# Four loads of the attention stage put behind group 4's transposing transfers (one-layer hybrid decoder step)

## The chip, the cores and the metric

The kernel runs on one core of a Trainium2 chip. The time is device microseconds from start to end of the program on that core, the median of the runs shown. TensorE is called PE, VectorE DVE, ScalarE ACT, GpSimd POOL and SyncE SP, as in the profile. All data is fp32; the large products are made of three fp32r passes (high times high, high times low, low times high).

## The reference, cut to what matters

```python
def _layer(x, ..., prompt):
    h = _rmsnorm(x, g_pre)
    z = h @ w_in                     # gates, conv inputs, queries, keys, values, memory queries
    ...
    conv = conv_w[0] * up[:, 0:t] + conv_w[1] * up[:, 1:t + 1] + conv_w[2] * up[:, 2:t + 2]
    out_a = jax.nn.silu(cg) * cb * conv
    ...
    out_b = jax.nn.silu(ag) * o_b    # o_b: sliding-window attention, window 128, a sink logit per head
    out_c = jax.nn.silu(mg) * o_c    # o_c: attention of 4 heads into 256 memory tokens
    y = jnp.concatenate([out_a, out_b, out_c], axis=-1) @ w_out
    return x + _rmsnorm(y, g_post), ...
```

There are 4096 prompt tokens and 64 sample tokens, a model width of 1024, 8 window heads over 2 key-value heads and 4 memory heads, all of head dimension 64.

## The kernel before, in words

The first part of the program, up to about 940 us, is the input projection. It leaves its products in DRAM: queries, keys and memory queries as high and low halves in `qd`, values in `vn`, and the gated convolution rows and gates in `md` (the "mix" rows, which the attention results multiply).

The second part runs over 33 blocks of output rows. **Block** i is 128 tokens; its output projection is 48 matmuls, 24 for each half of the 1024 columns (`y_0`, then `y_1`, line 1661). Queries, keys and mix rows are loaded by **chunks** of 256 tokens, two blocks each. The attention itself is done by **groups** of 128 tokens, group g belonging to chunk g // 2. Between the matmuls of block i the program places one attention step, `values_and_scores(i)`: the scores of group i + 3 (tiles `ws` and `xs`, matmuls at line 1128), then the values of group i + 1 (tile `pv`, same line), then the softmax of group i + 3 on DVE and ACT. The order on every engine is the order in which this code is written, the two DMA-issuing engines SP and POOL included.

What one group passes through after its softmax, and by which engine:

- `turn_band` and `turn_cross` (lines 1338 and 1342) transpose the weights in 32 x 32 squares on DVE. `turn_cross` then sends sixteen **transposing transfers** of 64 KB (`w<-s`, line 1345), which put the squares in their transposed places. For groups 3 and 4 the eight with odd k are kept in a list (`moves`) and are issued on POOL a little later, the eight with even k on SP at once. From group 5 on all sixteen are on SP.
- `masks` (line 1361, POOL) clears what lies outside the window. The values need its result.
- The values need also the chunk's mix rows (`load_mix`, line 1174, 1 MB into the tile `place` or `mix`; the product at lines 1375 and 1406 reads them) and two 128-token pieces of the values (`half_load`, line 1181, 64 KB, tiles `vh`).

The queries of a chunk are loaded by POOL in two halves, `load_queries(0)` and `load_queries(1)` (line 1166, tile `q<-qd`, 768 KB each: the high halves and the low ones); the keys by `load_keys` (line 1160, `kst<-qd`, 384 KB). Scores of a group need both halves of its chunk's queries from their first matmuls on.

A block's end is split in two tails that are placed in the next step: `tail(0)` computes the row's factor (`yst`; a power on POOL at line 1682), and `tail(1)` scales and adds the residual row `xr` (loaded by `block.load`, line 1616) and stores it (`o_yp<-xr`). For block 1 the scale and add are one DVE instruction at line 1697. The accumulator `y_1` of a block shares the PSUM tile `pv` with the values of the groups, and `y_0` shares a bank with the first scores; both are released by DVE's product with the gain (`yn`, line 1668) and ACT's square (line 1669).

Each kind of queue, SP's and POOL's, signals its transfers on eight semaphores in turn. A transfer waits on its engine for the transfer that used the same semaphore before it, which is the one eight places ahead of it in that kind of queue.

Of the kernel before, what the change touches and what calls it, by code (L numbers as in the profile page):

```python
# [26 lines left out]
NCH = 4096 // CT  # L27
# [24 lines left out]
def hybrid_layer(ctx: ExitStack, tc: tile.TileContext, a: dict):  # L52
# [1030 lines left out]
    chunks = {}  # L1083
# [23 lines left out]
    def psum(bank, name):  # L1107

        if ps is None:
            return third["ps"].tile([P, 512], F32, tag="m", name=name)  # L1110
        return ps[bank].tile([P, 512], F32, tag="b", name=name)
# [71 lines left out]
    class Group:  # L1183
# [32 lines left out]
        def scores(self):  # L1216
            self.open_scores()
            bands = [psum(n, f"ws{self.b}_{n}").rearrange("p (h k) -> p h k", h=2) for n in ((1, 2, 5, 4) if self.b == 4 else range(4))]
            cross_bank = lambda hh: psum(hh if self.b == 4 else 4 + hh, f"xs{self.b}_{hh}").rearrange("p (j k) -> p j k", j=2)
            if self.b != 4:  # L1220
                cross = [cross_bank(hh) for hh in range(2)]
            self.bands(bands[:2], 0)
            if self.b == 5:
                for fn in groups[4].moves:
                    fn()
            tail(0)
            if self.b == 4:
                turn(1, 3)
            loads = query_loads(self.b // 2 + 2)[:1] if self.b % 2 and self.b > 3 else query_loads(self.b // 2 + 1)[1:] if self.b > 4 else ()
            if self.b == 5:  # L1230
                loads.pop(0)()
            if self.b == 4:
                for fn in groups[3].moves:
                    fn()
                blocks[1].load()
                chunk_load(3)
            self.bands(bands[2:], 1)
            if self.b == 4:
                cross = [cross_bank(hh) for hh in range(2)]
            self.crosses(cross)  # L1240
            for fn in loads[:1]:
                fn()
            if self.b not in (4, 5):
                tail(1)
            for fn in loads[1:]:
                fn()
            if self.b == 3:
                blocks[1].split(0)
            self.band_softmax()
            return cross  # L1250
# [190 lines left out]
    def tail(part):  # L1441
        if part < len(tails):
            tails[part]()
        if part:
            tails.clear()

    def turn(part, g):
        if 3 <= g < 2 * NCH:
            (groups[g].turn_band, groups[g].turn_cross, groups[g].masks)[part]()

    def query_loads(c):
        if c >= NCH:
            return ()
        if c not in chunks:
            chunks[c] = Chunk(c)
        return [chunks[c].load_keys, lambda: chunks[c].load_queries(0), lambda: chunks[c].load_queries(1)]

    def chunk_load(c):
        for fn in query_loads(c):
            fn()  # L1460
# [255 lines left out]
    def events_of(i, block):  # L1716

        ev = {}

        def at(p, k, fn, *args):  # L1720
            ev.setdefault((p, k), []).append(lambda: fn(*args))

        if i < 2:
            at(1, 0, weights, i + 3)
        if i == 1:
            at(0, 0, turn, 0, 3)
        if i == 2:
            at(0, 0, turn, 0, 4)
            at(0, 0, turn, 1, 4)
        at(0, {0: 3, 1: 4}.get(i, 0), values_and_scores, i)  # L1730
        if i > 1:
            ev.setdefault((0, 0), []).insert(0, block.load)
        if i == 30:
            at(0, 5, blocks[32].split)
            at(1, 1, blocks[31].split)
            at(1, 6, blocks[31].load)
        if i % 2 == 0 and 2 < i < 2 * NCH - 2:
            at(0, 3, lambda: chunks[i // 2 + 1].load_mix())
        if i != 1:
            at(1, 1, turn, 2, i + 2)  # L1740
        if i == 1:
            at(0, 5, lambda: chunks[2].load_mix())
            at(0, 6, turn, 2, 3)
        if i > 0 and i + 3 < 2 * NCH:
            at(0, 5, half_load, i + 3)
        if i > 1:
            at(1, 2, turn, 0, i + 3)
            at(1, 2, turn, 1, i + 3)
        if i:
            if i + 1 < len(blocks) and blocks[i + 1].b != 32:  # L1750
                at(*((1, 3) if i < 28 else (0, 6)), blocks[i + 1].split, *((1,) if i == 1 else ()))
        for (n, p, k), stage in sample.items():
            if n == i:
                at(p, k, next, stage, None)
        return ev

    for i, block in enumerate(blocks):
        if block.b == 32:
            tail(0)
            tail(1)  # L1760
            blocks[32].load()
            for stage in (mem0, mem1, window):
                for _ in stage:
                    pass
        block.run(i == len(blocks) - 1, events_of(i, block) if i < 31 else {})
# [107 lines left out]
```

## Time and profile before

| | us |
|---|---|
| median of 3 runs (1471.61 to 1475.16) | 1474.47 |
| the profiled execution's own time | 1468.87 |
| its span, first to last instruction | 1467.1 |
| PE busy (matmuls) | 1453.7 |
| DVE busy | 1209.0 |
| ACT busy | 757.2 |
| POOL busy | 447.5 |

The 1.77 us between the profiled execution's time and its span lie before the first and after the last instruction. The mean granted TensorE clock is 0.999. The span is that of PE with few gaps: 13.4 us in which no matmul is under way. Times within the trace are given in us from the span's start.

### The profile page before, as it was taken

Reading aid. Unit: us, or ns where it says so; the run is one execution under the profiler, and the core shown is the slowest. Engines: PE = TensorE matmul, PEld = TensorE weight load, DVE = VectorE, ACT = ScalarE, POOL = GpSimd, SP = SyncE. Lnnn points to the kernel's source line nnn. Section 1 sums busy time; section 2 is a strip of 40 time slices with the busy share of each in tenths; the row PEclk is TensorE's granted clock in tenths of the full one; section 3 lists DMA queues with packets and bytes.
Section 4 is the critical chain, followed back from the end, with each engine's and each line's share of the span. In section 5 each row is a group of like instructions: output and inputs, shape, how many; then the busy total and the mean of one; then the engine's idle time right before and its main releaser. Section 6 shows DMA issues by size and latency. Waiting matters only on the chain.

```text
span 1467.1 us, 30934 instructions
## 1 busy us (share of the span) xinstructions
PE 1453.7 (99%) x11457; PEld 1335.7 (91%) x11457; DVE 1209.0 (82%) x1897; ACT 757.2 (52%) x1869; POOL 447.5 (31%) x622
## 2 busy tenths in 40 slices
PE   9999999999999999999999999999999999999998
PEld 9999999999999999999999999977777777777776
DVE  6779878899998877799677777988898889898853
ACT  6776655566522222244445544656656655655542
POOL 0222323312300000000002224265556566556561
PEclk9999999999999999999999999999999999999999
DMA  9989999887865644475977968999989898988772
GB/s 272 188 244 221 294 264 272 247 283 237 234 220 171 216 130 127 139 282 138 329 265 227 292 217 276 316 230 234 246 219 222 217 257 221 244 219 234 230 221 102
DMA packets 211980, 337.27 MB, mean 230 GB/s; under 512 B 55285, under 2 KB 125941, under 8 KB 211797
## 3 DMA queue, kind: packets, MB, share of 16 engines
q1 hardware_dynamic: 158901, 225.89, 52.0%
q0 software_dynamic: 44144, 78.68, 21.3%
q10 hardware_dynamic: 8784, 30.72, 6.8%
q8 instruction: 91, 1.49, 0.5%
q14 instruction: 60, 0.49, 0.1%
HBM read 192.48 MB, written 110.15 MB: 206 GB/s over the span
## 4 chain that ended last, share of the span: by engine, by line
PE 87%; DMA 5%; DVE 3%; SPq 2%; issue 1%; ACT 1%; POOL 1%; ACTq 0%; DVEq 0%; POOLq 0%
PE c L383 60%; PE y L1661 18%; PE pv L1128 4%; PE ws L1128 2%; SPq L1345 2%; DMA mix<-md 1%; DMA q<-qd 1%; PE xs L1128 1%; DMA qd<-z 1%; PE mem_acc L810 1%; DMA o_yp<-xr 1%; ACT s L1296 0%; DMA w<-s 0%; DMA xr<-in_x_p 0%; DMA vh<-vn 0%
## 5 line engine op out<-in xcount | busy, mean ns | idle before, releaser
L1661 PE MATMUL y<-wo,mh 128*128 128x512 f32 (+1 forms) x1040 | 328.7, 391 | 0.0
L390 DVE TENSOR_TENSOR z<-c,z 128x520 f32<-128x520 f32 (+1 forms) x308 | 193.2, 643 | 66.0 <-PE c L383 64.7
L1661 PEld LDWEIGHTS y<-wo,mh 128*128 128x128 f32 x1040 | 194.2, 188 | 52.4 <-DVE wmx L1286 5.0
L1661 PE MATMUL y<-wo,ml 128*128 128x512 f32 (+1 forms) x520 | 201.1, 387 | 0.0
L1330 POOL TENSOR_SCALAR s<-s,xrd 128x256 f32<-128x256 f32 x124 | 58.3, 482 | 199.5 <-DVE xrd L1325 193.9
L1661 PEld LDWEIGHTS y<-wo,ml 128*128 128x128 f32 x520 | 97.8, 188 | 18.5
L1296 ACT ACTIVATE s<-s,wnm 128x128 f32<-128x128 f32 x256 | 98.7, 387 | 0.0
L756 POOL MEMSET negs<- 128x1 f32 x1 | 0.1, 100 | 285.1 <-DMA md<-cacc 285.1
L1273 ACT COPY s<-ws 128x256 f32<-128x256 f32 x128 | 41.2, 378 | 76.4 <-PE ws L1128 66.1
L1691 POOL TENSOR_TENSOR xr<-yn,xr 128x1024 f32<-128x1024 f32 x29 | 69.4, 2394 | 17.9 <-ACT yn L1690 17.7
L1361 POOL TENSOR_SCALAR_AFFINE_SELECT wd<-w 128x512 f32<-128x512 f32 x64 | 59.4, 928 | 36.0 <-DMA w<-s 19.6
L1669 ACT ACTIVATE y<-y 128x512 f32<-128x512 f32 (+1 forms) x66 | 38.6, 585 | 60.8 <-DVE yn L1668 60.5
L1128 PEld LDWEIGHTS ws<-kst,q 64*128 64x128 f32 x768 | 47.7, 186 | 12.1 <-issue 9.2
L1319 ACT ACTIVATE s<-xs,xnm 128x256 f32<-128x256 f32 x128 | 58.0, 459 | 0.0
L1668 DVE TENSOR_TENSOR yn<-y,gpost 128x512 f32<-128x512 f32 (+1 forms) x66 | 44.7, 678 | 16.1 <-PE y L1661 15.0
L1361 POOL TENSOR_SCALAR_AFFINE_SELECT w<-w 128x512 f32<-128x512 f32 x64 | 56.5, 902 | 2.2
L1128 PE MATMUL ws<-kst,q 64*128 64x256 f32 x768 | 55.0, 288 | 1.0 <-ACT y L1669 1.0
L1277 DVE COPY_PREDICATED s<-wmask,ws 128x256 f32<-128x256 uint8 x124 | 47.9, 440 | 8.9 <-ACT s L1273 6.5
L392 ACT COPY z<-c 128x520 f32<-128x520 f32 (+1 forms) x44 | 24.3, 555 | 58.8 <-PE c L383 54.6
L296 ACT ACTIVATE nat<-nat 104x1024 f32<-104x1024 f32 x40 | 42.3, 1057 | 21.8 <-DMA nat<-in_x_p 21.8
L1296 ACT ACTIVATION_READ_ACCUMULATOR s<-s,wnm 128x1 f32 x256 | 47.9, 187 | 0.0
L187 POOL DMA_DIRECT2D md<-th x48 | 26.3, 549 | 70.2 <-DVE th L444 38.5
(968 smaller groups left out, 4970.9 us busy)
## 6 DMA issues: line engine op xcount, KB each, us to landing
w<-s SPq DMA_DIRECT2D x456, 64.0 KB
q<-qd POOLq DMA_DIRECT2D x32, 768.0 KB
xr<-in_x_p SPq DMA_DIRECT2D x32, 512.0 KB
nat<-in_x_p SPq DMA_DIRECT2D x39, 416.0 KB
o_yp<-xr SPq DMA_DIRECT2D x31, 512.0 KB
md<-th POOLq DMA_DIRECT2D x48, 260.0 KB
qd<-zh SPq DMA_DIRECT2D x48, 260.0 KB
qd<-z SPq DMA_DIRECT2D x48, 260.0 KB
```

What stands on the lines that cost most here:

```text
L296: S.activation(t[:RG], t[:RG], AF.Square, accum_out=r[:RG, i : i + 1])
L383: TE.matmul(bank[:, :HW], l, r, start=first and i == 0, stop=last and i == 3 * KH - 1)
L390: add = lambda dst, other: V.tensor_tensor(dst, c, other, op=ALU.add)
L1128: ins = TE.matmul(o, w, x, **kw)
L1277: V.copy_predicated(to, squares(third["wmask"]), squares(s3[:, :, 0:P]))
L1296: S.activation(sm[:, h], sm[:, h], AF.Exp, bias=nm[:, h : h + 1], scale=SCALE, accum_out=den[:, h : h + 1])
L1319: S.activation(p[:, i], s[:, i].rearrange("p (a k j) -> p a k j", a=2, k=4), AF.Exp, bias=nm[:, i : i + 1], scale=SCALE, accum_out=den[:, ...
L1330: G.tensor_scalar(p[:, i], p[:, i], rd[:, i : i + 1], 0.5, op0=ALU.mult, op1=ALU.mult)
L1361: G.affine_select(out, src, pattern=[[32 * sign, 2], [0, 8], [sign, 32]], compare_op=op, fill=0.0, base=base * sign, channel_multiplier=-s ...
L1661: TE.matmul(acc, self.hl[l][:, k], wo[k][c0 // 512][:, r, c0 % 512 : c0 % 512 + c1 - c0], start=j == 0, stop=j == passes * KT - 1)
L1668: V.tensor_tensor(yn[:m, c0:c1], acc[:m], gpost[0][:m, c0:c1], op=ALU.mult)
L1691: total = G.tensor_tensor(self.xr, yn, self.xr, op=ALU.add)
```

## The change

Five edits, all in the steps of blocks 1 and 2:

- `load_queries(1)` of chunk 3 was issued on POOL in group 4's scores (step 1). It is now issued in group 5's scores (step 2), behind group 4's eight transfers on POOL.
- `load_keys` of chunk 4 was issued at that place in group 5's scores; it is now issued after the cross scores of that group.
- `load_mix` of chunk 2 and `half_load(4)` were issued on SP in step 1. They are now issued at the start of step 2, behind group 4's eight transfers on SP.
- `block.load` of block 2 (its residual row) was SP's first instruction of step 2, ahead of group 4's transfers. It is now behind them and behind the two loads above.
- No other step issues anything at another place.

```diff
@@ Group.scores
             if self.b == 5:
-                loads.pop(0)()
+                chunks[3].load_queries(1)
             if self.b == 4:
                 for fn in groups[3].moves:
                     fn()
                 blocks[1].load()
-                chunk_load(3)
+                for fn in query_loads(3)[:2]:
+                    fn()
@@ events_of
         if i == 2:
             at(0, 0, turn, 0, 4)
             at(0, 0, turn, 1, 4)
+            at(0, 0, half_load, 4)
+            at(0, 0, lambda: chunks[2].load_mix())
+            at(0, 0, block.load)
         at(0, {0: 3, 1: 4}.get(i, 0), values_and_scores, i)
-        if i > 1:
+        if i > 2:
             ev.setdefault((0, 0), []).insert(0, block.load)
...
         if i == 1:
-            at(0, 5, lambda: chunks[2].load_mix())
             at(0, 6, turn, 2, 3)
-        if i > 0 and i + 3 < 2 * NCH:
+        if i > 1 and i + 3 < 2 * NCH:
             at(0, 5, half_load, i + 3)
```

SP's queue, from group 3's transfers to block 1's end, before (`w_12385` is group 3's, `w_12563` group 4's; `xr_12402` and `xr_12559` are the residual rows of blocks 1 and 2, `xr_12190` block 0's; `place` takes chunk 2's mix rows):

```order
L1345 DMA w_12385<-s_12204 32x512 x8
L1616 DMA xr_12402<-in_x_p 128x1024
L1698 DMA o_yp<-xr_12190 128x1024
L1174 DMA place<-md 128x8x256
L1181 DMA vh_12499<-vn 128x128
L1616 DMA xr_12559<-in_x_p 128x1024
L1345 DMA w_12563<-s_12361 32x512 x8
L1698 DMA o_yp<-xr_12402 128x1024
L1181 DMA vh_12714<-vn 128x128
```

The same stretch of SP's queue in the changed kernel, whose line numbers are one higher there (`w_12557` is group 4's, `xr_12569` block 2's residual row):

```order
L1346 DMA w_12385<-s_12204 32x512 x8
L1617 DMA xr_12402<-in_x_p 128x1024
L1699 DMA o_yp<-xr_12190 128x1024
L1346 DMA w_12557<-s_12361 32x512 x8
L1181 DMA vh_12566<-vn 128x128
L1174 DMA place<-md 128x8x256
L1617 DMA xr_12569<-in_x_p 128x1024
L1699 DMA o_yp<-xr_12402 128x1024
L1181 DMA vh_12714<-vn 128x128
```

Three loads moved from ahead of group 4's eight transfers to behind them; nothing else changed places.

POOL's queue before, from group 3's transfers to the loads of chunk 4's keys (`q_12406` and `kst_12404` are chunk 3's, `kst_12606` chunk 4's; `yst_12346` is block 1's factor):

```order
L1345 DMA w_12385<-s_12204 32x512 x8
L1160 DMA kst_12404<-qd 128x2x384
L1166 DMA q_12406<-qd 128x6x256 x2
L1361 AFFINE_SELECT wd_12504<-w_12385 128x512
L1361 AFFINE_SELECT wd_12504<-w_12385 64x512
L1361 AFFINE_SELECT w_12385<-w_12385 128x2x256 x2
L1345 DMA w_12563<-s_12361 32x512 x8
L1682 TENSOR_TENSOR yst_12346<-yst_12346,mhalf 128x1
L1160 DMA kst_12606<-qd 128x2x384
```

The same stretch of POOL's queue in the changed kernel (`kst_12634` is chunk 4's):

```order
L1346 DMA w_12385<-s_12204 32x512 x8
L1160 DMA kst_12404<-qd 128x2x384
L1166 DMA q_12406<-qd 128x6x256
L1362 AFFINE_SELECT wd_12500<-w_12385 128x512
L1362 AFFINE_SELECT wd_12500<-w_12385 64x512
L1362 AFFINE_SELECT w_12385<-w_12385 128x2x256 x2
L1346 DMA w_12557<-s_12361 32x512 x8
L1683 TENSOR_TENSOR yst_12346<-yst_12346,mhalf 128x1
L1166 DMA q_12406<-qd 128x6x256
L1160 DMA kst_12634<-qd 128x2x384
```

The second half of chunk 3's queries moved from ahead of group 4's eight transfers to behind them and behind block 1's factor; the transfer eight places ahead of the last of the eight is now the first half of the queries and no longer the second.

## The prediction

> **What bounds the kernel now.** I read first how busy each engine is: PE's matmuls cover 99% of the span, so only what lets PE wait, or adds to it, can move the time.
>
> ```profile
> PE 1453.7 (99%) x11457; PEld 1335.7 (91%) x11457; DVE 1209.0 (82%) x1897; ACT 757.2 (52%) x1869; POOL 447.5 (31%) x622
> ```
>
> The span is 1467.1 us, so 13.4 us hold no matmul. The view of waits, for PE alone, tells which of them have a releaser (engine, line waited for, us in total, times, longest).
>
> ```profile
> PE pv L1128 <- ACT y L1669: 3.8, 4, 2.3
> PE ws L1128 <- ACT y L1669: 1.0, 1, 1.0
> ```
>
> The first scores of a group and the values of a group wait for ACT's square of a block's output, which frees the PSUM tile. Where this happens is read in order of time from PE's weight loads: the score and value rows of steps 2 to 6, that is the scores of groups 5 to 9. The number ahead of the arrow is the idle time before the row.
>
> ```profile
> 964.55 1.49 PEld L1128 LDWEIGHTS ws<-kst,q 64*128 64x128 f32 x24 [0.35 <-ACT s L1328]
> 981.59 1.49 PEld L1128 LDWEIGHTS ws<-kst,q 64*128 64x128 f32 x24 [1.45 <-ACT y L1669]
> 986.30 0.85 PEld L1128 LDWEIGHTS pv<-w,mv 128*64 128x64 f32 x16 [2.49 <-ACT y L1669]
> 999.90 1.49 PEld L1128 LDWEIGHTS ws<-kst,q 64*128 64x128 f32 x24 [0.35 <-issue]
> 1002.68 0.85 PEld L1128 LDWEIGHTS pv<-w,mv 128*64 128x64 f32 x16 [0.57 <-ACT y L1669]
> 1016.30 1.49 PEld L1128 LDWEIGHTS ws<-kst,q 64*128 64x128 f32 x24 [0.35 <-issue]
> 1018.64 0.85 PEld L1128 LDWEIGHTS pv<-w,mv 128*64 128x64 f32 x16
> 1032.25 1.49 PEld L1128 LDWEIGHTS ws<-kst,q 64*128 64x128 f32 x24 [0.35 <-issue]
> ```
>
> From 1016.30 to 1032.25 a step without a wait takes 15.95 us, and its values start 2.34 us after its scores. The three steps before it take 17.04, 18.31 and 16.40 us, so they lose 1.09, 2.36 and 0.45 us: **3.90 us in all**. That is the most that this change can gain at the place it touches.
>
> What makes ACT late there stands in the chain that ended last (start, us, what).
>
> ```profile
> 960.23 15.34 DMA q<-qd
> ...
> 975.84 0.25 POOL w L1345
> ...
> 976.35 0.59 POOL yst L1682
> 976.97 1.29 DVE xr L1697
> ...
> 980.17 0.60 DVE yn L1668
> 980.85 0.47 ACT y L1669
> ```
>
> The second half of chunk 3's queries, issued at 960.23, lands at 975.57. POOL's last transposing transfer of group 4 waits for it, because it stands eight software transfers behind it; behind it on POOL stands block 1's factor, behind that on DVE the residual addition at line 1697, and behind that the `yn` that frees block 2's accumulators.
>
> **The change part by part.** First POOL (start, length, instruction, idle before it).
>
> ```profile
> 968.22 3.51 POOL L1345 DMA_DIRECT2D w<-s  x7 [0.76 <-DVE s L1277]
> 975.84 0.50 POOL L1345 DMA_DIRECT2D w<-s  x1 [4.12 <-DMA q<-qd]
> 980.22 1.84 POOL L1330 TENSOR_SCALAR s<-s,xrd 128x256 f32<-128x256 f32 x4 [2.56 <-DVE xrd L1325]
> 983.08 2.36 POOL L1361 TENSOR_SCALAR_AFFINE_SELECT wd<-w 128x512 f32<-128x512 f32 x2 [1.02 <-DMA w<-s]
> 985.51 1.40 POOL L1361 TENSOR_SCALAR_AFFINE_SELECT w<-w 128x512 f32<-128x512 f32 x2
> 987.41 0.91 POOL L1166 DMA_DIRECT2D q<-qd  x1
> 991.07 0.86 POOL L1166 DMA_DIRECT2D q<-qd  x1
> ```
>
> With the second query half gone from ahead, the eighth transfer waits for the first half, which was issued one place earlier in the old order. Keys and first half are 1152 of the 1920 KB that had landed after 15.34 us, so by the same rate they are in about 9.2 us after 960.23, at 969.4 and likely earlier, since the other half and the mix rows no longer compete. The eight transfers then run from 968.22 for 8 x 0.50 us to 972.2, block 1's factor is ready 0.59 us later at 972.8, and the moved query load is issued at 972.8. It adds nothing to POOL's work. The keys of chunk 4 come one place later in POOL's order, 0.9 us, for scores that begin at 1016.30; I take nothing for them.
>
> Now DVE, and in the last row ACT.
>
> ```profile
> 973.09 0.17 DVE L1313 TENSOR_SCALAR xnm<-xmx 128x2 f32<-128x2 f32 x1
> 976.97 1.29 DVE L1697 SCALAR_TENSOR_TENSOR xr<-yn,yst,xr 128x1024 f32<-128x1024 f32 x1 [3.71 <-POOL yst L1682]
> 980.09 0.67 DVE L1668 TENSOR_TENSOR yn<-y,gpost 128x512 f32<-128x512 f32 x1
> 983.26 1.60 DVE L1636 TENSOR_TENSOR ml<-mix,mh 128x1024 fp32r<-128x1024 f32 x1
> 984.79 0.68 DVE L1668 TENSOR_TENSOR yn<-y,gpost 128x512 f32<-128x512 f32 x1
> ```
>
> ```profile
> 985.56 0.58 ACT L1669 ACTIVATE y<-y 128x512 f32<-128x512 f32 x1 [1.65 <-DVE yn L1668]
> ```
>
> DVE is free at 973.26, and the factor is there at 972.8. The whole row of DVE work behind it moves up by the 3.71 us that DVE now waits. The first `yn` goes from 980.09 to 976.4 (block 2's first half ends on PE half an output projection before 980.5, at about 975, so its data is there), and the first scores of group 6 find their bank free: **1.09 us** gained. The second `yn` goes from 984.79 to 981.1, after PE's end of block 2 at 964.55 + 15.95 = 980.50. The values started 1.51 us after that `yn` (986.30 less 984.79), so they may start at 982.6; unhindered PE comes to them at 980.50 + 2.34 = 982.84. That is **2.36 us** more, with 0.25 us in hand. What is late next is the same square one step on, the 0.45 us before 1002.68; its DVE chain moves with PE, and I leave it.
>
> The masks must not become the wait instead. POOL's scaling at 980.22 moves up by 3.71 to 976.5 and ends at 978.4; masks of 3.8 us follow until 982.2, while PE reads the first masked tile 0.85 us into the values, at 983.7. For that group 4's transfers must land by 978.4. On SP they are freed as follows.
>
> ```profile
> 961.19 0.65 SPq L1174 DMA_DIRECT2D place<-md  x1
> 961.89 4.26 SPq L1181 DMA_DIRECT2D vh<-vn  x1
> 969.41 0.33 SPq L1616 DMA_DIRECT2D xr<-in_x_p  x1
> 970.11 10.56 SPq L1345 DMA_DIRECT2D w<-s  x8
> 983.41 10.04 SPq L1345 DMA_DIRECT2D w<-s  x16
> ```
>
> Before, SP held block 2's load until 969.41 and then took 10.56 us for eight transfers. Group 5's sixteen took 10.04, or 0.63 each. In the new order the eight start when DVE has transposed, near POOL's 968.2, and take 8 x 0.63 = 5.0 us, to 973.2: 7.4 us earlier than 980.67. POOL's `wd` at 983.08 shows the old ones landed 2.4 us after the last issue; so about 975.6, 2.8 us before they are needed. I take nothing for the masks; the bounds are nothing and, if they landed as late as before, the old 2.4 us.
>
> The three loads now behind them: the 64 KB of values have from 973.2 to 983.7. The mix rows are issued at about 973.8 and needed by DVE after the values, past 985. SP's next instruction stood 4.26 us behind the mix rows' issue, so block 2's residual row goes out at about 978; it is needed only at block 2's end, by a POOL addition near 986. Nothing on PE waits for that addition directly. I take 0 for the three; the upper bound is 15.34 us to land, as the query half took, which puts the mix rows at 989: DVE some 2 us late in a step where it has more slack than that before the next `yn`.
>
> The one load with a near deadline is **the second query half**: issued at 972.8, needed by the first scores of group 6 at 980.50, so 7.7 us. Here the queues' traffic helps (packets, MB, share of the sixteen engines): the first two rows are 970 to 975, when this half ran beside the mix rows; the last two are the software queue in 996 to 997 and 997 to 998, when the same load for chunk 4, issued at 991.07, came to its end.
>
> ```profile
> q1 hardware_dynamic: 922, 0.95, 68.9%
> q0 software_dynamic: 549, 0.69, 50.2%
> ...
> q0 software_dynamic: 118, 0.11, 63.1%
> q0 software_dynamic: 2, 0.00, 1.5%
> ```
>
> The later load took 6 us from issue to end: by that row it lands at 978.8. At the 0.138 MB per us of the shared stretch its 0.79 MB need 5.7 us, plus the time to its first packet. The far end is the 15.34 us of the old order, where those 1152 KB stood in front. I take 6 us, the row of a load with nothing large ahead of it, and so no wait; 15.34 us would mean 988.1 and a wait of 7.6 us. The Trainium skill (DMA: Bandwidth & Descriptors, Anatomy of one DMA) gives a software transfer 2.0 us plus its bytes at 436 GB/s, an estimate of 3.8 us for this one. By that it lands at 976.6 and the sum is the same; the row at 991.07 with its 6 us does not agree, and decides.
>
> **The sum**: 1.09 + 2.36 = 3.45 us less. Against the profiled execution that is 1468.87 - 3.45 = 1465.4. That execution was 5.6 us under the median of the runs shown, so for the median I say 1474.47 - 3.45 = **1471.0**.
>
> **The rivals.**
> *The query half lands late.* Between 980.50 and 983.95 it eats the gain and the time lies between 1471.0 and 1474.5. For it: it shares with the mix rows and group 4's last transfers, and has 1.7 us in hand. The Trainium skill (DMA: Bandwidth & Descriptors, Rules for kernel authors) says to issue a transfer early and wait for it late; the change does the opposite with this one, and by that rule the time would go this way. The trace bears it out only for what something waits for soon: this is the one such load.
> *Slower.* The same load landing after 983.95, 11.1 us past its issue, costs more than both waits returned; at the old 15.34 us the time is 1474.47 + 7.6 - 3.45 = 1478.6. Against it: no row shows such a load that slow without another one ahead of it.
> *The wait stays.* If POOL's eighth transfer found the first query half still under way until 975, or the masks took the place of the square, the time would be 1473.5 to 1474.5. Against it: the 9.2 us above.
> *More than the profile shows.* The runs shown are 2.7 to 6.3 us slower than the profiled one. If part of that is these same waits, longer, up to 3 us more go: 1468.
>
> **How the numbers follow.** Forecast 0.64, late but not slower 0.14, slower 0.08, wait stays 0.07, more 0.07. A measurement of this kernel tells about 0.3% (4.4 us) from no change, and the forecast's 3.45 us are 0.23%, so it counts as within, but scatter may carry a seventh of it over. Faster by over 0.3%: 0.07 + 0.09 = 0.16. Slower by over 0.3%: the far part of the slower case and some scatter, 0.06. Within: 0.78. The range takes in the profiled basis, 1465.4, and the late landings up to about 1477.
>
> **What would show it.** Right: POOL's eight transfers unbroken from about 968, line 1698 (1697 before) on DVE near 973.3, score rows of groups 6 and 7 some 16 us apart, SP's eight in 5 us. Wrong: PE or its weight loads waiting for `q<-qd` at 980.5, POOL waiting for a transfer before the eighth, or masks that end after 983.7.

## The result and the profile after

The changed kernel takes **1468.21 us** (median of 19 runs, 1465.55 to 1471.74); the kernel before, run beside it, 1472.16 (19 runs, 1468.93 to 1478.06). The ratio is 0.9969, 95% interval 0.9959 to 0.9979: 3.1 to 6.0 us faster, 4.6 in the middle. The two medians themselves lie 3.95 us apart.

The two profiled executions have spans of 1467.1 and 1465.5 us. Their difference of 1.6 us isn't the change's: the scores of group 5 begin at 964.55 in the profile of before and at 968.64 in this one, and these 4.1 us are there already in the input projection (the weight load `c<-hi_7T,w_0A` that starts at 930.12 in one starts at 934.22 in the other), before any line that the change touches. In the other ten profiles of this study (two of them of the unchanged kernel) the scores begin between 967.8 and 972.0, so the first profile of before had a quick start. What the change does is read from there on, over the three steps that waited; behind them this profile is 1.8 us shorter again, by waits of later steps that differ from profile to profile. PE's weight loads of the changed kernel, scores and values of groups 5 to 9 (start, length, instruction, idle time before it):

```profile
968.64 1.49 PEld L1128 LDWEIGHTS ws<-kst,q 64*128 64x128 f32 x24 [0.35 <-ACT s L1329]
984.59 1.49 PEld L1128 LDWEIGHTS ws<-kst,q 64*128 64x128 f32 x24 [0.35 <-issue]
986.93 0.85 PEld L1128 LDWEIGHTS pv<-w,mv 128*64 128x64 f32 x16
1000.54 1.49 PEld L1128 LDWEIGHTS ws<-kst,q 64*128 64x128 f32 x24 [0.35 <-issue]
1002.88 0.85 PEld L1128 LDWEIGHTS pv<-w,mv 128*64 128x64 f32 x16
1016.46 1.49 PEld L1128 LDWEIGHTS ws<-kst,q 64*128 64x128 f32 x24 [0.35 <-issue]
```

The three steps take 15.95, 15.95 and 15.92 us: none of the three waits is left, where before they cost 1.09, 2.36 and 0.45 us. Below, **lost** means what these three steps take beyond 3 x 15.95 = 47.85 us: 3.90 before, nothing here (1016.46 - 968.64 = 47.82).

POOL of the changed kernel (same columns):

```profile
972.31 3.99 POOL L1346 DMA_DIRECT2D w<-s  x8 [0.75 <-DVE s L1278]
976.31 0.57 POOL L1683 TENSOR_TENSOR yst<-yst,mhalf 128x1 f32<-128x1 f32 x1
976.85 0.89 POOL L1166 DMA_DIRECT2D q<-qd  x1
980.52 1.84 POOL L1331 TENSOR_SCALAR s<-s,xrd 128x256 f32<-128x256 f32 x4 [2.05 <-DVE xrd L1326]
982.33 1.50 POOL L1362 TENSOR_SCALAR_AFFINE_SELECT wd<-w 128x512 f32<-128x512 f32 x2
983.89 2.26 POOL L1362 TENSOR_SCALAR_AFFINE_SELECT w<-w 128x512 f32<-128x512 f32 x2
```

The eight transfers run without a break, block 1's factor stands right behind them, and the masks end at 986.15, 17.5 us after the scores of group 5 (before: 986.91, 22.4 us). SP, DVE and ACT of the same kernel:

```profile
971.79 5.07 SPq L1346 DMA_DIRECT2D w<-s  x8
976.91 0.84 SPq L1181 DMA_DIRECT2D vh<-vn  x1
977.79 0.45 SPq L1174 DMA_DIRECT2D place<-md  x1
978.28 0.58 SPq L1617 DMA_DIRECT2D xr<-in_x_p  x1
983.71 12.69 SPq L1346 DMA_DIRECT2D w<-s  x16
```

```profile
977.27 1.28 DVE L1698 SCALAR_TENSOR_TENSOR xr<-yn,yst,xr 128x1024 f32<-128x1024 f32 x1
980.39 0.67 DVE L1669 TENSOR_TENSOR yn<-y,gpost 128x512 f32<-128x512 f32 x1
984.82 0.68 DVE L1669 TENSOR_TENSOR yn<-y,gpost 128x512 f32<-128x512 f32 x1
```

```profile
985.60 0.65 ACT L1274 COPY s<-ws 128x256 f32<-128x256 f32 x2 [2.82 <-PE ws L1128]
986.14 0.60 ACT L1670 ACTIVATE y<-y 128x512 f32<-128x512 f32 x1
```

SP's eight take 5.07 us in place of 10.56. Block 2's residual row (`xr`) goes out 9.6 us after the scores of group 5. The second query half is issued 8.21 us after the scores of group 5; the software queue moved its bytes until about 982.0 (0.04, 0.16, 0.33 and 0.24 MB in the four microseconds from 978), so it took 5.2 us and was there 2.6 us before the scores that read it. ACT shows a thing to remember: ahead of the square that frees the values' bank stands ACT's **copy of group 6's scores into `s`**. Here it waits for PE alone.

### The profile page after: what moved, and what is told of

Same layout as the page of the kernel before. It is cut to its first block, busy times and chain, and to the rows that moved or that the text cites. A ratio compares the mean times of both kernels' runs of the same rounds, so it can differ in the third digit from the quotient of the medians.

```text
span 1465.5 us, 30938 instructions
## 1 busy us (share of the span) xinstructions
PE 1453.8 (99%) x11457; PEld 1335.6 (91%) x11457; DVE 1206.9 (82%) x1897; ACT 756.5 (52%) x1869; POOL 448.6 (31%) x622
## 4 chain that ended last, share of the span: by engine, by line
PE 83%; DMA 7%; issue 3%; SPq 2%; DVE 2%; ACT 2%; POOL 1%; ACTq 0%; POOLq 0%; DVEq 0%
PE c L383 50%; PE y L1662 22%; PE pv L1128 5%; PE ws L1128 3%; SPq L1346 2%; PE xs L1128 1%; DMA mix<-md 1%; DMA x_0B<-in_xt 1%; PE mem_acc L810 1%; DMA md<-th 1%; DMA w<-s 1%; DMA wr_2A<-in_w_in 1%; DMA wr_3S<-sd6S 1%; DMA vd<-v 0%; DMA x_1B<-in_xt 0%
## 5 line engine op out<-in xcount | busy, mean ns | idle before, releaser
L1669 DVE TENSOR_TENSOR yn<-y,gpost 128x512 f32<-128x512 f32 (+1 forms) x66 | 44.7, 678 | 16.2 <-PE y L1662 14.7
```

The costliest lines, as they stand in the source:

```text
L1669: V.tensor_tensor(yn[:m, c0:c1], acc[:m], gpost[0][:m, c0:c1], op=ALU.mult)
```

## The experiments

The reason on record had one chain: query half, POOL's eighth transfer, factor, DVE, square. Four theories were set against each other. *Held factor*: that chain is all. *Two causes*: behind it stands a second one, group 4's transfers held on SP (the sixth of the eight stands eight places behind the mix rows), that keeps the second wait up alone. *Lighter queues*: what counts is that fewer bytes are under way, not the order on an engine. *Late query half*: the moved load is near its limit, and its place decides. Lost, from one profile of each kernel, and the gain by the timed runs (from the ratio, of 1472 us):

| kernel | us (runs) | before beside it | ratio, 95% | gain us | lost us |
|---|---|---|---|---|---|
| before, three profiles | | | | | 3.90, 5.04, 4.58 |
| changed | 1468.21 (19) | 1472.16 | 0.9969, 0.9959 to 0.9979 | 4.6 | -0.03 |
| changed, again | 1467.90 (12) | 1472.63 | 0.9967, 0.9953 to 0.9981 | 4.9 | 0.25 |
| POOL's edits alone | 1470.09 (12) | 1472.02 | 0.9991, 0.9974 to 1.0007 | 1.3 | 3.18 |
| SP's edits alone | 1470.53 (12) | 1472.02 | 0.9993, 0.9978 to 1.0008 | 1.0 | 1.24 |
| before, factor ahead | 1471.67 (12) | 1472.02 | 0.9997, 0.9983 to 1.0010 | 0.4 | 3.54 |
| SP's edits, factor ahead | 1468.77 (12) | 1472.63 | 0.9970, 0.9955 to 0.9984 | 4.4 | 0.36 |
| changed, residual row ahead | 1469.67 (12) | 1472.05 | 0.9975, 0.9956 to 0.9993 | 3.7 | 1.33 |
| changed, mix rows ahead | 1471.04 (12) | 1472.05 | 0.9991, 0.9974 to 1.0008 | 1.3 | 6.32 |
| changed, query half later | 1478.48 (12) | 1472.05 | 1.0037, 1.0022 to 1.0052 | -5.4 | 9.8 |

In the last row all of it lies in one step: the three take 15.98, 25.72 and 15.94 us. The intervals of *POOL's edits alone*, *SP's edits alone*, *before, factor ahead* and *changed, mix rows ahead* take in no change at all.

### POOL's edits alone

```diff
             if self.b == 5:
-                loads.pop(0)()
+                chunks[3].load_queries(1)
...
-                chunk_load(3)
+                for fn in query_loads(3)[:2]:
+                    fn()
```

> Only POOL's part: the second query half of chunk 3 behind group 4's transfers and block 1's factor; SP's three loads where they were before. Theory H (held factor): the waits come from POOL's eighth transfer standing behind that query half, so POOL's eight run unbroken, line 1697 on DVE comes at about 973.3 of the trace's time (3.7 us earlier) and the wait of 1.09 us at group 6's scores goes. Under H alone the 2.36 us at its values go as well: 3.45 us gained. Rival T (late transfers): SP's eight are still held behind block 2's load and the mix rows and land near 983, so the masks end near 986.8 and PE waits for POOL's masks instead of ACT's square, some 2 to 3 us in the values of group 4: about 1 us gained in all. Rival D (lighter queues): the gain goes with the bytes moved out of step 1, 0.79 of 2.4 MB: about 1.2 us, spread over both waits, with no new wait for masks.

The factor is free early (line 1698 on DVE 8.6 us after the scores of group 5, as in the changed kernel, 12.4 before), and still 3.18 us are lost. PE's weight loads, then POOL's masks with the wait before them:

```profile
986.62 1.37 PEld L1128 LDWEIGHTS ws<-kst,q 64*128 64x128 f32 x22 [1.60 <-DMA q<-qd]
990.09 0.85 PEld L1128 LDWEIGHTS pv<-w,mv 128*64 128x64 f32 x16 [1.39 <-ACT y L1670]
```

```profile
978.37 0.89 POOL L1166 DMA_DIRECT2D q<-qd  x1 [1.25 <-DMA w<-s]
988.62 1.51 POOL L1362 TENSOR_SCALAR_AFFINE_SELECT wd<-w 128x512 f32<-128x512 f32 x2 [6.04 <-DMA w<-s]
```

SP's eight transfers, and ACT's copy of group 6's scores:

```profile
975.11 7.73 SPq L1346 DMA_DIRECT2D w<-s  x8
```

```profile
988.80 0.65 ACT L1274 COPY s<-ws 128x256 f32<-128x256 f32 x2 [5.80 <-DMA w<-s]
```

With the mix rows and block 2's load still ahead, the query half is itself issued 1.25 us late and lands 8.1 us after its issue: PE waits for it, 1.60 us. Group 4's transfers hold the masks until 988.62 and ACT's copy, with the square behind it, until 988.80, and for that square PE waits 1.39 us more. So POOL's edits alone trade one wait for two others. Theory H alone, 3.45 us gained, fails; T has the size (0.7 us less lost than before, 1.3 by the timed runs), though PE waits through the copy and not only for the masks. The last of SP's eight was issued by 982.84, so these transfers came late by more than their issue: the moved query half was on its way beside them.

### SP's edits alone

```diff
+            at(0, 0, half_load, 4)
+            at(0, 0, lambda: chunks[2].load_mix())
+            at(0, 0, block.load)
...
-        if i > 1:
+        if i > 2:
...
-            at(0, 5, lambda: chunks[2].load_mix())
...
-        if i > 0 and i + 3 < 2 * NCH:
+        if i > 1 and i + 3 < 2 * NCH:
```

> Only SP's part: mix rows, value half and block 2's residual row behind group 4's transfers; the second query half stays in step 1 on POOL. Theory H: the eighth transfer still waits for that query half. Without the mix rows beside it the half lands some 3 us sooner, near 972.5, so POOL is held about 1 us and not 4; the scores of group 6 find no wait and the values wait some 0.5 us: 2.5 to 3 us gained, with POOL's wait ahead of the eighth transfer still in the trace. If the half lands as late as before (975.6), the wait stays whole and nothing is gained. Rival T: SP's eight go out in 5 us and land near 976, which by T is the cause, so 3.4 us gained whatever POOL waits. Rival D: 1.6 of 2.4 MB, 2.3 us gained.

```profile
991.25 0.85 PEld L1128 LDWEIGHTS pv<-w,mv 128*64 128x64 f32 x16 [1.35 <-ACT y L1669]
```

```profile
975.39 3.51 POOL L1345 DMA_DIRECT2D w<-s  x7 [0.74 <-DVE s L1277]
981.06 0.50 POOL L1345 DMA_DIRECT2D w<-s  x1 [2.17 <-DMA q<-qd]
```

Of the three kernels with one cause taken away this loses least in its profile: 1.24 us. The eighth transfer still waits for the query half, but 2.17 us in place of 4.12 (the half no longer runs beside the mix rows); DVE reaches line 1697 at 10.5 us after the scores in place of 12.4, and the first wait is gone. ACT's copy no longer waits for a transfer here, and the square behind it waits 1.16 us for DVE's `yn`, so the held factor costs something by itself: T, by which nothing would be left, fails, and H expected 0.5 us in place of 1.24. The timed gain, 1.0 us with an interval from 3.2 faster to 1.2 slower, doesn't confirm the size: this execution alone has a stretch at a lower clock at 80 to 100 us (0.91 granted), far from the change, and 8 of its 12 executions have a mean clock below 0.999.

### The kernel before, with the factor ahead of the moves

```diff
             self.bands(bands[:2], 0)
+            tail(0)
             if self.b == 5:
                 for fn in groups[4].moves:
                     fn()
-            tail(0)
```

> The kernel before with one change: in group 5's scores block 1's factor (tail 0) is written ahead of group 4's eight transfers on POOL, so that it no longer stands behind the eighth. All loads stay where they were. Theory H: line 1697 on DVE starts near 973.3 although POOL's eighth transfer still waits until 975.8, and no square of block 2 is late. T: group 4's transfers still land near 983 and the masks end near 986.8, so PE waits about 3 us for POOL's masks inside the values of group 4, and the whole gain is under 1 us. H without T: 3.45 us. D: no byte moves, so nothing is gained and the waits on the square stay.

No byte moves elsewhere, and the factor no longer stands behind POOL's eighth transfer. The first wait is gone (15.95 us), line 1697 starts 8.6 us after the scores, and the second `yn` starts in time, at 984.42. But PE waits longer for the second. PE's list of waits (releaser, us in total, times, longest), then the row in order of time, ACT and POOL:

```profile
PE pv L1128 <- DMA w<-s: 3.2, 1, 3.2
```

```profile
989.83 0.85 PEld L1128 LDWEIGHTS pv<-w,mv 128*64 128x64 f32 x16 [3.45 <-ACT y L1669]
```

```profile
988.53 0.65 ACT L1273 COPY s<-ws 128x256 f32<-128x256 f32 x2 [6.16 <-DMA vh<-vn]
989.07 0.60 ACT L1669 ACTIVATE y<-y 128x512 f32<-128x512 f32 x1
```

```profile
988.35 1.51 POOL L1361 TENSOR_SCALAR_AFFINE_SELECT wd<-w 128x512 f32<-128x512 f32 x2 [6.24 <-DMA o_yp<-xr]
```

```profile
974.57 9.80 SPq L1345 DMA_DIRECT2D w<-s  x8
```

This is the second cause by itself. SP's eight transfers are late (issued over 9.80 us). They read the squares from `s`, and ACT's copy of group 6's scores writes that tile: it waits 6.16 us until they have landed, and the square that PE needs is the next instruction on ACT. (The rows of ACT and POOL name a 64 KB load and a 512 KB store that SP issued right behind the eight; neither touches `s` or `w`. PE's row names `w<-s`, and so does the row of the copy in POOL's edits alone.)

In the first profile of before the copy was released 18.7 us after the scores of group 5 and the second `yn` started at 20.2; here it is 20.3 and 16.2. So the two causes ended close together there, the factor's being the later. *Held factor* alone falls: its removal gains 0.4 us by the timed runs and 0.4 to 1.5 in the profile. *Lighter queues* falls for the first wait, which went with no byte moved. For the second it stays open: SP's edits both change the order and move 1.6 MB away from group 4's transfers, which landed 4.0 us after the last one's issue here and 2.4 in the first profile of before, and no run separates the two. The expectation put the second wait on the masks; the copy on ACT starts its wait with them and was not foreseen.

### SP's edits and the factor ahead

This has the two causes removed and leaves the query half early, where it was: the diffs of the last two experiments together.

> SP's part of the change, the second query half still in step 1, and block 1's factor written ahead of group 4's eight transfers on POOL. SP's part alone lost 1.2 us in steps 3 to 5, with POOL's eighth transfer waiting 2.17 us for the query half and the factor behind it. Theory H: that 1.2 us is the held factor; with the factor ahead, line 1697 on DVE starts 3 to 4 us sooner against the scores of group 5 and steps 3 to 5 lose 0 to 0.3 us, as in the changed kernel, although the eighth transfer still waits. Rival T: the eighth transfer itself, landing 2 us late, holds the masks or ACT's copy, and 1 us stays. If H holds this version equals the changed kernel, about 4.5 us under the kernel before.

```profile
972.82 0.57 POOL L1682 TENSOR_TENSOR yst<-yst,mhalf 128x1 f32<-128x1 f32 x1 [1.01 <-DVE yst L1681]
977.87 0.50 POOL L1345 DMA_DIRECT2D w<-s  x1 [1.00 <-DMA q<-qd]
982.80 1.51 POOL L1361 TENSOR_SCALAR_AFFINE_SELECT wd<-w 128x512 f32<-128x512 f32 x2
```

0.36 us are lost (0 to 0.3 expected) and the time is 0.9970 of before: within the noise as fast as the changed kernel, 0.9967 beside it. That the query half moves is thus not needed; what is needed is that the factor doesn't wait behind it. T, by which 1 us would stay, fails. *Two causes* stands on this run and on the profiles of the halves; by the timed runs alone, the intervals of this kernel and of SP's edits alone still overlap.

### The changed kernel, block 2's residual row ahead again

```diff
-            at(0, 0, block.load)
         at(0, {0: 3, 1: 4}.get(i, 0), values_and_scores, i)
-        if i > 2:
+        if i > 1:
             ev.setdefault((0, 0), []).insert(0, block.load)
```

> The changed kernel with only block 2's residual row back ahead of group 4's transfers on SP. Theory: what holds SP's eight is the mix rows (a transfer waits for the one eight places ahead), and block 2's row only until block 0's store has landed, which is about 1.5 us past the transposes. So SP's eight start 1.5 to 2.5 us later, go out in about 5 us and the masks still end in time: the same as the changed kernel within 0.5 us, no wait over 0.5 us in steps 3 to 5. Rival: block 2's row is what matters, and the waits at group 4's values come back, 2 us or more.

```profile
976.30 5.08 SPq L1346 DMA_DIRECT2D w<-s  x8
985.38 15.56 SPq L1346 DMA_DIRECT2D w<-s  x16
```

```profile
1004.08 0.65 ACT L1274 COPY s<-ws 128x256 f32<-128x256 f32 x2 [4.52 <-DMA w<-s]
1004.61 0.61 ACT L1670 ACTIVATE y<-y 128x512 f32<-128x512 f32 x1
```

The one 512 KB load ahead starts group 4's eight 6.0 us after the scores of group 5 in place of 3.2, though they then take the same 5.08 us. The loss comes one group later and by the same path: group 5's sixteen take 15.56 us, and ACT's copy, with the square behind it, waits for them. The expectation, no wait over 0.5 us, missed: 1.33 us are lost. Why the sixteen take longer isn't shown. The interval (1.0 to 6.5 us gained) can't tell it from the changed kernel.

### The changed kernel, mix rows ahead again

```diff
-            at(0, 0, half_load, 4)
-            at(0, 0, lambda: chunks[2].load_mix())
...
+            at(0, 5, lambda: chunks[2].load_mix())
...
-        if i > 1 and i + 3 < 2 * NCH:
+        if i > 0 and i + 3 < 2 * NCH:
```

> The changed kernel with only the mix rows and the value half back in step 1. Theory: SP's sixth transfer again waits for the mix rows, which land sooner than before (no second query half beside them), by about 972 to 973 of the first profile's time; so SP's eight end near 976 to 977 and the masks near 983 to 984, at the edge: a wait of 0 to 1 us in group 4's values, a gain of 2.9 to 3.9 us on the kernel before. Rival: the mix rows hold SP as long as before, ACT's copy and the masks come 3 us late and the gain falls to 1 us, as with POOL's part alone.

```profile
982.08 0.89 POOL L1166 DMA_DIRECT2D q<-qd  x1 [2.14 <-DMA w<-s]
```

```profile
991.55 2.42 PEld L1128 LDWEIGHTS ws<-kst,q 64*128 64x128 f32 x22 [3.69 <-DMA q<-qd]
```

The expectation, a wait of 0 to 1 us, missed. The query half is issued 2.14 us later, because the transfer eight places ahead of it, group 4's first on POOL, is late (SP's queue moves 1.00 MB from 976 to 979, the mix rows among it); it then needs 9.4 us. The profiled execution was the slowest of the twelve (1477.79 against a median of 1471.04), so 6.32 us is not typical; 3.69 us of it is PE's wait, and much of the rest a lower clock behind it (0.50 granted from 991 to 997). The gain by the ratio, 1.3 us, still lies 3.3 us under the change's, though the two intervals touch. In this profile at least, the late query half is safe only with the mix rows behind the transfers.

### The changed kernel, query half behind the masks

```diff
             if self.b == 5:
-                chunks[3].load_queries(1)
+                pass
...
+        if i == 2:
+            at(1, 1, lambda: chunks[3].load_queries(1))
```

> The changed kernel with the second query half issued still later, behind group 4's masks (about 5 us later on POOL). It prices the rival of a late query half. In the changed kernel's trace it was issued at 976.85, its traffic ended near 982 and group 6's scores started at 984.59, so 2.6 us were in hand. Issued near 986.2 and landing 5 to 6 us later, at 991 to 992, it makes PE wait 6.5 to 7.5 us at group 6's scores, with the query load as releaser, where the changed kernel waits 0 and the kernel before 3.90. Theory H with the clock rival C below: 3 us slower than before from the wait alone (1475.0), and if an idle PE of over 2.4 us also halves the clock for some 3.5 us, as one of two profiles of the kernel before shows, 1.7 us more, 1476.7. Without C: 1475.0 and a clock of 1.00 behind the wait.

```profile
991.83 2.42 PEld L1128 LDWEIGHTS ws<-kst,q 64*128 64x128 f32 x22 [7.49 <-DMA q<-qd]
```

Three stretches of the same kernel (stretch, us, busy time and count of PE, PE's loads, DVE, ACT, POOL; then the granted clock, the DMA share and GB/s):

```profile
986.00:991.00 5.00, 0.00 (x0) 0.00 (x0) 0.00 (x0) 0.00 (x0) 0.52 (x1) 0.57 1.03 239
991.00:996.00 5.00, 4.17 (x36) 3.95 (x38) 1.97 (x6) 2.40 (x7) 1.11 (x2) 0.50 0.62 136
996.00:998.00 2.00, 2.00 (x24) 1.64 (x22) 1.97 (x2) 0.64 (x1) 1.55 (x2) 0.78 0.67 238
```

Issued 9.3 us later than in the changed kernel (17.5 us after the scores of group 5 against 8.2), the half lands 6.2 us after its issue and PE waits 7.49 us. The clock then stands at 0.50 until about 997, which adds some 2.3 us: 9.8 lost, 5.4 us slower than before by the ratio (6.4 by the medians). The clock fell as theory C had it, for longer than the 3.5 us it allowed, so its 1476.7 is 1.8 us too low. The Trainium skill (DMA: Bandwidth & Descriptors, Rules for kernel authors) says to issue early and wait late; here breaking that rule has its price. The changed kernel breaks it too, and stays clear of the price by the 2.6 us read above.

### The kernel before, twice more

> The kernel before, unchanged, for a second profile. The waits at steps 3 to 5 come from the written order and the queues, so all theories expect them again within about 1 us of 3.90 us. If they are much longer here, the measured gain above 3.45 us is these same waits, longer in most runs than in the first profile; if they are the same, the rest of the gain is elsewhere.

> The kernel before, unchanged, a third profile, for how often the wait of about 2.4 us at group 4's values halves the TensorE clock. Theory C (clock): the first profile waited 2.36 us there with the clock at 1.00, the second lost 4.04 us in the same step with the clock at 0.50 to 0.65 for 4 us; so the loss of steps 3 to 5 is 3.9 or about 5 us, and nothing between. Rival: the second profile's dip was an accident and the loss is 3.9 us with the clock at 1.00.

Scores and values of group 6 in the second profile of before, and stretches of it:

```profile
985.31 1.48 PEld L1128 LDWEIGHTS ws<-kst,q 64*128 64x128 f32 x24 [1.32 <-ACT y L1669]
990.13 1.57 PEld L1128 LDWEIGHTS pv<-w,mv 128*64 128x64 f32 x16 [2.62 <-ACT y L1669]
```

```profile
988.00:990.00 2.00, 0.00 (x0) 0.00 (x0) 1.98 (x4) 0.61 (x3) 1.93 (x2) 0.99 0.41 98
990.00:992.00 2.00, 1.87 (x18) 1.87 (x20) 1.80 (x4) 1.29 (x4) 2.00 (x4) 0.50 0.41 102
992.00:994.00 2.00, 2.00 (x18) 0.81 (x14) 1.93 (x3) 0.47 (x1) 1.60 (x2) 0.65 0.62 106
```

In the third, POOL's eighth transfer:

```profile
984.00 0.50 POOL L1345 DMA_DIRECT2D w<-s  x1 [4.78 <-DMA q<-qd]
```

The first two waits stand in both; the third is 0.46 us in the third profile and absent in the second. In the second profile the clock falls to half in the gap before the values, from 990.0 to about 993.4, which makes 5.04 us; in the third the query half lands later still (12.0 us after the scores of group 5, 11.3 in the first), the first wait grows to 1.76 us and the sum to 4.58, with the clock at 1.00. So theory C's "nothing between" missed: the loss varies without the clock too.

### The changed kernel again

> The changed kernel again, unchanged, beside the version above, for a second profile of it and a time from the same chip. The first profile lost nothing in steps 3 to 5 (15.95, 15.95, 15.92 us); three profiles of the kernel before lost 3.90, 5.04 and 4.58. If the loss is 0 again, the gain is 4 to 5 us, as measured (0.9969); if the query half is late in some runs (it had 2.6 us in hand), a wait for it shows here and the gain is smaller.

0.25 us are lost, and the ratio, 0.9967, repeats the first. In all, the changed kernel has a mean clock below 0.999 in 3 of 31 executions, and the kernel before in 37 of the 81 beside the experiments. Among the executions at 0.999 and above of this comparison the medians are 1471.54 (11) and 1467.39 (10), 4.15 us apart; over all of them 1472.63 and 1467.90, 4.73 apart. So some 0.6 us of the gain goes with executions in which the clock fell, and the trace of one of them shows it falling in this wait. That it falls there in all of them isn't shown: SP's edits alone had it fall elsewhere.

## Why the prediction was right, and where it was off

- **Place and mechanism**: the place is right, and the mechanism is right for the first wait and incomplete for the second. The forecast was 3.45 us less, and the interval is 3.1 to 6.0; the 0.31% of the ratio lies just past the 0.3% within which the prediction put 0.78, on the side that it gave 0.16. The absolute number, 1471.0, missed 1468.21 by 2.8 us, of which 2.3 is the base: the 19 runs of before have a median of 1472.16, the three shown had 1474.47.
- **POOL, first step**: right to 0.1 us. After the scores of group 5 the factor was said to be ready at 8.25 us and the query half to be issued there; it was issued at 8.21. Line 1698 was said for 8.71 and came at 8.63.
- **The first wait, 1.09 us**: right; and the factor ahead of the moves shows the cause alone.
- **The second wait, 2.36 us**: it went as said, but the step that gave it to DVE's `yn` alone was incomplete. The factor ahead of the moves has that `yn` in time and a wait of 3.45 us, through ACT's copy into `s`. The sum held because the change also frees SP, which the prediction counted at nothing ("I take nothing for the masks; the bounds are nothing and ... the old 2.4 us"). The working saw that SP's eight would come sooner, but only as a danger to the masks that stays covered; it had no term for the copy, and that the same edits cover it was luck. Without them (POOL's edits alone) 3.18 us stayed lost.
- **The third wait, "I leave it"**: counted at 0. It was 0.45, 0 and 0.46 us in the three profiles of before and 0 and 0.22 in the two of the change, so that the change removes it isn't shown.
- **"3.90 us in all ... the most that this change can gain"**: too low as a bound. It was one execution of three; the mean of the three is 4.5 us. The case called *more than the profile shows*, with a chance of 0.07 and 1468, is what happened in part, by longer waits in the third profile and a lower clock in the second.
- **The query half**: issue to end 5.2 us, said 6; in hand 2.6 us, said 1.7. *Late query half* did not occur, but the two kernels with it late show that the limit is near.
- **SP's eight**: 5.07 us, said 5.0. Masks: end 17.5 us after the scores, said 17.65. Block 2's residual row was said to go out near 978, 13.4 us after the scores, held behind the mix rows as before; it went out at 9.6, since in the new order nothing held SP there. Group 5's sixteen take 12.69 us (10.04 before) beside the three loads; not foreseen. In this profile that has no price; with the residual row ahead they take 15.56, and the step behind loses 1.13.

## What to carry to other kernels

Where an engine's wait names one releaser, look for what would be late next without it: here two causes stood behind one wait, and by the timed runs the removal of either alone returned 0.4 to 1.3 us of the 4.6, each with an interval that takes in zero. A transfer that must wait for an older one (4.12 us on POOL here) holds every compute instruction behind it on the issuing engine, so a small operation that others wait for goes ahead of it; beside SP's edits that replaced the move of a 768 KB load. And one profile of a wait is one draw: two more of the same kernel put the ceiling 0.7 and 1.1 us higher.

## What the runs showed of the hardware

The clock can fall in a short gap. PE's matmuls at the second wait, first in the second profile of before, then in the kernel before with the factor ahead, with a stretch of the latter behind it (columns as above):

```profile
990.13 1.98 PE L1128 MATMUL pv<-w,mv 128*64 128x128 f32 x16 [2.42 <-ACT y L1669]
```

```profile
989.83 1.09 PE L1128 MATMUL pv<-w,mv 128*64 128x128 f32 x16 [3.24 <-DMA w<-s]
```

```profile
990.00:991.00 1.00, 1.00 (x20) 0.88 (x18) 0.92 (x4) 0.32 (x2) 1.00 (x2) 1.00 0.53 129
```

After 2.42 us without a matmul the sixteen take 1.98 us at a granted clock of 0.50; after 3.24 us they take 1.09 at 1.00, as they do after 2.29 and 2.31 us in the first and third profile of before. So the length of the gap alone doesn't decide, and what does isn't shown. The Trainium skill (TensorE: Matmul & The Clock Gate, What's actually happening) lets the clock fall after an idle window of about 3.4 us; the fall after 2.42 us doesn't agree with that as a lower bound, and the trace decides. With the gaps of 3.5 us (mix rows ahead) and 7.3 us (query half behind the masks) it fell too, and came back 5 to 6 us after PE's restart.

The load of 768 KB took 5.2 us from issue to end in the changed kernel, 6.2 with the query half behind the masks, 8.1 in the kernel with POOL's edits alone and 9.4 with the mix rows ahead. What of this is the traffic beside it and what the transfers ahead of it on its own queue, no run separates.
